# VectorE takes GpSimd's elementwise work, and the first half's low-rank projection moves into its first two tiles

## The chip, the cores and the metric

One Trainium2 chip, one of its cores. The metric is the time of one execution on the device in microseconds (us): 1757.95 us is the median of three runs of the kernel before (1757.51 to 1762.42). The profile is one further execution, of 1757.43 us.

## What is computed

One layer of a hybrid decoder in float32, for a prompt of 1024 tokens with 16 meta tokens ahead, and for 8 sequences of 8 new tokens. Cut to what the change touches:

```python
def rmsnorm(x, w):
    var = jnp.mean(xf * xf, axis=-1, keepdims=True)
    return xf * lax.rsqrt(var + EPS) * w

h = rmsnorm(x, norm_pre)                                    # [tokens, 2048]
q_a, k_a, v_a, gate_a, q_g, k_g, v_g, gate_g, z_g = jnp.split(h @ w_in, SPLIT_POINTS, axis=-1)
log_f = jax.nn.log_sigmoid(z_g @ w_a2 + b_a) / GLA_NORMALIZER   # z_g: 16 columns, the low-rank projection
# (A) softmax attention in a window of 128, gated by silu(gate_a)
# (B) gated linear attention (GLA, 4 heads) with decays from log_f, normalised, gated by silu(gate_g)
x + rmsnorm(concat(A, B) @ w_out, norm_post)
```

The norm's factor 1/sqrt(var) belongs to a token, and so to a column of the transposed arrays that the kernel works on. It commutes with the projection: the kernel projects `x * norm_pre` and multiplies each result by the token's factor `rs`.

## The kernel before

**Layout and halves.** Activations are transposed: 128 features on the partitions, tokens on the free axis. Tokens fall into a first half (A, 512) and a second half (B, 592). `in_half` runs for A, then for B; the output projection follows for A (`out_first`) and for B (`out_second`, twice 296 columns).

**The projections.** `proj` (L343) makes one or two tiles of 128 output features. A tile is 16 contraction steps (kt) of three float32r matmuls at L358, because each operand is split in two parts, `whi`+`wlo` for the weights and `hh`+`hl` for the activations: `hh,whi`, `hl,whi`, `hh,wlo`. That is 48 matmuls a tile and column part. The activation parts of a half are made once, in the half's first `proj` call (`prep_x`, L215), which runs two tiles together: ScalarE makes `hh` (L201), VectorE `hl` (L202). The weights come in jobs of 8 kt (512 KB, tile `wraw`, 3 buffers). `convert` makes of each job two pieces of 4 kt: ScalarE casts `whi` (L322), VectorE subtracts for `wlo` (L324), 4 buffers each. `weights` keeps one job ahead of the one in use.

**The sum of squares.** In half A the same `prep_x` squares each x and adds it up in two sums, `acc[0]` for even kt and `acc[1]` for odd ones. GpSimd squares kt 0 and 1 (L229) and adds the even ones (L233), VectorE adds the odd ones (L233), ScalarE squares the others (L231). After the last matmul of the two tiles, `finish_norm` (L235) adds over the partitions on TensorE (L244), and `rstd` (L168) makes `rs`. Only then are the two tiles, q and k of the first GLA head, taken out of PSUM, multiplied by `rs` (`evac_rs`). Half B's sum is made during half A by `prepass` (L248), added on GpSimd (L259).

**The low-rank projection.** `zproj` (L368) then takes a weight job of its own, `wz` (304 KB), and makes 32 matmuls at L377 from all 16 `hh` and `hl`. Its result times `rs`, split again (`zT`), feeds the decays of every GLA head of the half (L671).

**What sets the order.** A scheduler places the program's instructions in each engine's queue; an engine works its queue off in that order and waits on semaphores. Attention (`attend`), GLA (`gla`) and side jobs (`setup_late`, `prepass`) are generators, of which `mid` and `end` run a step between projection calls, so their instructions lie between matmuls of L358. GpSimd's part of them before: the softmax's last multiplication (L529), the two multiplications of each level of a GLA head (`operands`, L737 and L738, after two exponentials of ScalarE), the last one of `silu` (L438), and those of L784, L812, L823 and L915. Its other work is memsets, copies of some columns, and six DMAs, among them two small-packet writes to DRAM for the bias tables (L140, L141).

## Time and profile before

| | |
|---|---|
| median of 3 runs | 1757.95 us (1757.51 to 1762.42) |
| the profiled execution | 1757.43 us, span 1755.6 us, mean granted TensorE clock 0.991 |
| TensorE busy, matmuls | 1716.6 us, 98% |
| TensorE busy, weight loads | 1552.1 us, 88% |
| VectorE busy | 1014.0 us, 58% |
| ScalarE busy | 741.9 us, 42% |
| GpSimd busy | 355.4 us, 20%, 332 instructions |

In the rows, PE is TensorE's matmuls, PEld its weight loads, DVE VectorE, ACT ScalarE, POOL GpSimd, SP the engine that issues the loads. A group's row gives line, engine, operation, out<-in tiles and shapes, count, busy time and mean duration, then the engine's idle time ahead of it and what ended that. A matmul's duration in the trace overlaps the next one's; the pace is read from one start to the next.

### The profile page before, as it was taken

Reading aid. Unit: us, or ns where it says so; the run is one execution under the profiler, and the core shown is the slowest. Engines: PE = TensorE matmul, PEld = TensorE weight load, DVE = VectorE, ACT = ScalarE, POOL = GpSimd, SP = SyncE. Lnnn points to the kernel's source line nnn. Section 1 sums busy time; section 2 is a strip of 40 time slices with the busy share of each in tenths; the row PEclk is TensorE's granted clock in tenths of the full one; section 3 lists DMA queues with packets and bytes.
Section 4 is the critical chain, followed back from the end, with each engine's and each line's share of the span. In section 5 each row is a group of like instructions: output and inputs, shape, how many; then the busy total and the mean of one; then the engine's idle time right before and its main releaser. Section 6 shows DMA issues by size and latency. Waiting matters only on the chain.

```text
span 1755.6 us, 28693 instructions
## 1 busy us (share of the span) xinstructions
PE 1716.6 (98%) x11068; PEld 1552.1 (88%) x11068; DVE 1014.0 (58%) x1993; ACT 741.9 (42%) x1603; POOL 355.4 (20%) x332
## 2 busy tenths in 40 slices
PE   7999999999999999999999999999999999999995
PEld 5778888888888999999999999999997788899995
DVE  7466675675656757435654564455656533585655
ACT  6344454353434534332443243343435333544442
POOL 3043253141114114211231022210521100000000
PEclk9999999999999999999999999999999999999998
DMA  6733433222233532313223231323225333686664
GB/s 212 146 97 111 132 115 105 93 83 94 88 96 108 175 121 70 101 64 113 82 67 102 81 115 60 102 77 107 79 77 199 104 99 102 224 262 222 208 217 159
DMA packets 85736, 213.61 MB, mean 122 GB/s; under 512 B 11504, under 2 KB 33936, under 8 KB 85568
## 3 DMA queue, kind: packets, MB, share of 16 engines
q1 hardware_dynamic: 82416, 204.90, 36.2%
q0 software_dynamic: 992, 4.46, 1.6%
q10 hardware_dynamic: 2192, 2.43, 0.4%
q8 instruction: 87, 1.43, 0.3%
q14 instruction: 49, 0.40, 0.1%
HBM read 186.32 MB, written 27.39 MB: 122 GB/s over the span
## 4 chain that ended last, share of the span: by engine, by line
PE 88%; DVE 4%; DMA 3%; ACT 2%; issue 1%; POOL 1%; SPq 0%; DVEq 0%; POOLq 0%; ACTq 0%
PE mm L358 76%; PE ps L521 2%; DMA wraw<-in_win 1%; PE ps L764 1%; PE ps L551 1%; PE ps L377 1%; PE ps L537 1%; PE ps L876 1%; DVE wlo L324 1%; PE ps L848 1%; PE ps L878 1%; PE ps L553 1%; ACT whi L322 0%; PE ps L187 0%; PE ps L923 0%
## 5 line engine op out<-in xcount | busy, mean ns | idle before, releaser
L358 PE MATMUL mm<-hh,whi 128*128 128x296 f32 (+2 forms) x2880 | 846.3, 333 | 8.5 <-ACT whi L322 6.0
L358 PE MATMUL mm<-hh,wlo 128*128 128x296 f32 (+2 forms) x2880 | 840.7, 331 | 2.6 <-DVE wlo L324 2.5
L358 PE MATMUL mm<-hl,whi 128*128 128x296 f32 (+2 forms) x2880 | 836.9, 330 | 2.1 <-DVE hl L202 1.6
L324 DVE TENSOR_TENSOR wlo<-wraw,whi 128x512 fp32r<-128x512 f32 x544 | 420.3, 778 | 444.4 <-ACT whi L322 432.1
L322 ACT CAST whi<-wraw 128x512 fp32r<-128x512 f32 x544 | 334.5, 619 | 785.6 <-PE mm L358 698.8
L358 PEld LDWEIGHTS mm<-hh,whi 128*128 128x128 f32 x2880 | 506.7, 189 | 51.5 <-ACT whi L322 7.7
L358 PEld LDWEIGHTS mm<-hh,wlo 128*128 128x128 f32 x2880 | 507.9, 189 | 43.0 <-DVE wlo L324 4.9
L358 PEld LDWEIGHTS mm<-hl,whi 128*128 128x128 f32 x2880 | 508.9, 189 | 39.6 <-DVE hl L202 3.1
L529 POOL TENSOR_TENSOR st<-st,den 128x512 f32<-128x512 f32 x32 | 44.3, 1386 | 350.0 <-ACT whi L322 260.3
L401 DVE TENSOR_TENSOR ft<-mm,rs 128x592 f32<-128x592 f32 (+2 forms) x60 | 43.6, 727 | 69.9 <-PE mm L358 67.2
L485 ACT ACTIVATE st<-st,nm 128x128 f32<-128x128 f32 (+1 forms) x140 | 54.7, 391 | 65.7 <-DVE nm L479 65.7
L737 POOL TENSOR_TENSOR ft<-ft 128x256 f32<-128x256 f32 (+2 forms) x48 | 53.0, 1104 | 142.1 <-ACT ft L735 142.1
L438 POOL TENSOR_TENSOR ft<-ft 128x496 f32<-128x496 f32 (+1 forms) x32 | 51.6, 1613 | 92.0 <-ACT ft L437 92.0
L738 POOL TENSOR_TENSOR ft<-ft 128x256 f32<-128x256 f32 (+2 forms) x48 | 50.0, 1041 | 1.4 <-ACT ft L736 1.4
L915 POOL TENSOR_TENSOR ft<-ft 128x496 f32<-128x496 f32 (+1 forms) x16 | 27.2, 1719 | 99.3 <-DVE ft L912 99.3
L540 DVE TENSOR_TENSOR pT<-ps,c_sides 128x512 f32<-128x512 f32 x64 | 41.3, 682 | 2.5 <-PE ps L537 2.3
L734 DVE TENSOR_TENSOR ft<-ft 128x512 f32<-128x512 f32 (+2 forms) x48 | 40.8, 859 | 0.0
L509 DVE TENSOR_TENSOR qst<-ft,qst 64x256 fp32r<-64x256 f32 x64 | 38.6, 603 | 2.5 <-ACT qst L508 0.6
L403 DVE SCALAR_TENSOR_TENSOR ft<-mm,rs 128x496 f32<-128x496 f32 (+1 forms) x24 | 17.4, 725 | 35.6 <-PE mm L358 35.4
L764 PEld LDWEIGHTS ps<-ft 128*126 128x126 f32 (+3 forms) x256 | 30.9, 187 | 6.1 <-POOL ft L738 4.6
L259 POOL TENSOR_TENSOR rs<-rs,ft 128x592 f32<-128x592 f32 x15 | 24.1, 1609 | 52.0 <-ACT ft L257 51.9
L764 PE MATMUL ps<-ft 128*126 128x64 f32 (+3 forms) x256 | 31.2, 267 | 3.2 <-POOL ft L738 3.2
(316 smaller groups left out, 1605.4 us busy)
## 6 DMA issues: line engine op xcount, KB each, us to landing
wraw<-in_win SPq DMA_DIRECT2D x174, 512.0 KB, 3.8
wraw<-in_wout SPq DMA_DIRECT2D x96, 512.0 KB, 4.4
ft<-in_xB SPq DMA_DIRECT2D x48, 296.0 KB, 4.2
ft<-mix SPq DMA_DIRECT2D x16, 296.0 KB, 6.3
ft<-in_xA SPq DMA_DIRECT2D x16, 256.0 KB, 5.6
ft<-in_state SPq DMA_DIRECT2D x16, 256.0 KB, 5.0
...
```

What stands on the lines that cost most here:

```text
L322: nc.scalar.copy(hi, r)
L324: nc.vector.tensor_tensor(lo, r, hi.bitcast(F32), ALU.subtract)
L358: nc.tensor.matmul(ps[:, j, :p1 - p0], w[:, k % 4, :], h[kt][:, p0:p1], start=(kt == 0 and a == 0), stop=(kt == KT - 1 and a == 2))
L401: self.nc.vector.tensor_tensor(o, src, r, ALU.mult)
L438: nc.gpsimd.tensor_tensor(x[:, :T], x[:, :T], t[:, :T], ALU.mult)
L485: nc.scalar.activation(s, s, AF.Exp, bias=nm[:R, j:j + 1], accum_out=den[:R, j:j + 1])
L529: nc.gpsimd.tensor_tensor(st, st, den.rearrange("p (v t) -> p v t", v=2).unsqueeze(3).to_broadcast([P, 2, 2, P]), ALU.mult)
L540: nc.vector.tensor_tensor(sb[:, j], pt, self.sides[:, j:j + 1].to_broadcast([P, 4, P]), ALU.mult)
L734: nc.vector.tensor_tensor(ev, bv, bv[:, :, h - 1:h].to_broadcast([P, ns, 2 * h]), ALU.subtract)
L737: nc.gpsimd.tensor_tensor(ev[:, :, h:], qv[:, :, h:], ev[:, :, h:], ALU.mult)
L738: nc.gpsimd.tensor_tensor(ev[:, :, :h], kv[:, :, :h], ev[:, :, :h], ALU.mult)
L764: nc.tensor.matmul(ps[:P - h, j * 64:(j + 1) * 64], xs[:, :P - h], xs.rearrange("p (s e) -> p s e", e=2 * h)[:, :, h:], start=True, stop=True)
```

## The change

All elementwise arithmetic of GpSimd (L259, L438, L501, L529, L613 to L618, L723, L724, L737, L738, L784, L812, L823, L902, L915) goes to VectorE, one word each. GpSimd keeps memsets, copies and its DMAs. In half A's first call, ScalarE makes all 16 squares, and VectorE adds them up at least three steps of kt behind (`add_square`). The weights of the low-rank projection are loaded once more at the start, ahead of x 2, and converted at once into buffers that are free then. Half A's first call becomes `first`: its two tiles carry the 32 matmuls of the low-rank projection as a third sum, two kt behind. The tiles q and k are copied out raw; the norm is finished within the next tile (v0), between its two jobs, and q, k and z are multiplied by `rs` then. Half B keeps the old form. In the diff, the engine's name alone changes in some 20 more places like the first.

```diff
@@ prepass
-                nc.gpsimd.tensor_tensor(acc[:, :T], acc[:, :T], x[:, :T], ALU.add)
+                nc.vector.tensor_tensor(acc[:, :T], acc[:, :T], x[:, :T], ALU.add)
...
@@ prep_x
-                a = self.acc[kt % 2][:, :T]
-                if kt < 2:
-                    nc.gpsimd.tensor_tensor(a, x[:, :T], x[:, :T], ALU.mult)
-                else:
-                    nc.scalar.activation(x[:, :T], x[:, :T], AF.Square)
-                    eng = nc.vector if kt % 2 else nc.gpsimd
-                    eng.tensor_tensor(a, a, x[:, :T], ALU.add)
+                sq = self.acc[kt] if kt < 2 else x
+                nc.scalar.activation(sq[:, :T], x[:, :T], AF.Square)
+                if kt >= 2:
+                    self.sqs.append((kt, x))
+                if len(self.sqs) > 3:
+                    self.add_square(T)
...
@@ start
+            if j == 0:
+                wz = self.sm([P, 2, 4, P], "pT", 1).rearrange("p a b c -> p (a b) c")
+                self.load_x(A, 2)
+                nc.sync.dma_start(out=wz.rearrange("p k m -> p (k m)")[:, :608], in_=self.i["wz"])
             self.load_x(A, 4 + 4 * j)
+        self.wz0 = self.convert_z(wz, [self.sm([P, 4, P], "A", 1).bitcast(F32R).rearrange("p k m -> p (k m)"),
+                                       self.sm([P, 2, 256], "qst", 1, F32R).rearrange("p k m -> p (k m)")])
...
@@ proj
+                if extra is not None:
+                    extra(kt)
             if c == 0:
+                if between is not None:
+                    between()
                 self.mid()
-        if pre is not None and name == "win" and H.i == 0:
-            self.finish_norm(H)
...
@@ first (new)
+        zs = self.ps()
+        lag = 2
+        def extra(kt):
+            if kt >= lag:
+                self.zstep(H, self.wz0, [zs], kt - lag)
+            if kt == KT - 1:
+                for k in range(KT - lag, KT):
+                    self.zstep(H, self.wz0, [zs], k)
...
+        self.proj(H, "win", [base, base + 1], [evac("q", o0, nc.scalar.copy), evac("k", 0, nc.vector.tensor_copy)],
+                  [H.asked, H.parts], pre=lambda kts: self.prep_x(H, kts), extra=extra)
...
+        def between():
+            self.finish_norm(H)
+            self.zfinish(H, [zs])
+            nc.vector.scalar_tensor_tensor(q[:, o0:T], q[:, o0:T], scale, self.rs[:, o0:T], op0=ALU.mult, op1=ALU.mult)
+            nc.vector.tensor_tensor(k[:, :T], k[:, :T], self.rs[:, :T], ALU.mult)
+            self.glas.append(self.gla(H, 0, self.zT, io))
...
+        self.proj(H, "win", [base + 2], [evac_v], between=between)
```

**TensorE, the last kt of the first two tiles.** Before, the two tiles end, and the sum of squares (L244) and the first two of 32 matmuls of the low-rank projection (L377) follow:

```order
L358 MATMUL mm<-hh,wlo 128x496
L358 MATMUL mm<-hh,whi 128x512
L358 MATMUL mm<-hl,whi 128x512
L358 MATMUL mm<-hh,wlo 128x512
L244 MATMUL ps<-st,ones 128x512 x2
L377 MATMUL ps<-hh,whi 128x512
L377 MATMUL ps<-hl,whi 128x512
```

Now, over one kt near the end of the two tiles (L377 is here the line of the tiles, L403 that of the low-rank projection, `qst` its converted weights):

```order
L403 MATMUL ps<-hh,qst 128x512
L403 MATMUL ps<-hl,qst 128x512
L377 MATMUL mm<-hh,whi 128x496
L377 MATMUL mm<-hl,whi 128x496
L377 MATMUL mm<-hh,wlo 128x496
L377 MATMUL mm<-hh,whi 128x512
L377 MATMUL mm<-hl,whi 128x512
L377 MATMUL mm<-hh,wlo 128x512
L403 MATMUL ps<-hh,qst 128x512
```

The low-rank matmuls stand among the tiles' own from the seventh place of the queue on; after the last kt six of them follow, then v0. The sum of squares stands in the middle of v0 (L251).

**VectorE, the same two tiles.** Before, from kt 7 to kt 13 (L202 `hl`, L324 `wlo`, L233 sum of squares):

```order
L202 SCALAR_TENSOR_TENSOR hl<-ft,wpre,hh 128x512
L324 TENSOR_TENSOR wlo<-wraw,whi 128x512 x2
L233 TENSOR_TENSOR st<-st,ft 128x512
L202 SCALAR_TENSOR_TENSOR hl<-ft,wpre,hh 128x512 x3
L233 TENSOR_TENSOR st<-st,ft 128x512
L202 SCALAR_TENSOR_TENSOR hl<-ft,wpre,hh 128x512 x3
```

Now, from kt 7 to kt 12 (L238 sum of squares, L343 `wlo`):

```order
L202 SCALAR_TENSOR_TENSOR hl<-ft,wpre,hh 128x512
L343 TENSOR_TENSOR wlo<-wraw,whi 128x512 x2
L238 TENSOR_TENSOR st<-st,ft 128x512 x2
L202 SCALAR_TENSOR_TENSOR hl<-ft,wpre,hh 128x512 x3
L238 TENSOR_TENSOR st<-st,ft 128x512
L202 SCALAR_TENSOR_TENSOR hl<-ft,wpre,hh 128x512
L238 TENSOR_TENSOR st<-st,ft 128x512
L202 SCALAR_TENSOR_TENSOR hl<-ft,wpre,hh 128x512
```

VectorE's queue holds 14 additions in place of 7. Of the 14, ten stand ahead of the last `hl`, against six of the 7 before.

**VectorE, the start of the first GLA head.** Before, VectorE had these between `wlo` pieces, and GpSimd the multiplications of the levels:

```order
L324 TENSOR_TENSOR wlo<-wraw,whi 128x512
L734 TENSOR_TENSOR ft<-ft 128x512
L324 TENSOR_TENSOR wlo<-wraw,whi 128x512
L786 TENSOR_TENSOR ft<-ft 128x512
L401 TENSOR_TENSOR ft<-mm,rs 128x496
```

Now (L764 is the old L734, L767 and L768 the multiplications of a level, L468 that of `silu`):

```order
L343 TENSOR_TENSOR wlo<-wraw,whi 128x512
L751 TENSOR_TENSOR ft<-ft 128x256
L753 TENSOR_TENSOR ft<-ft 128x256
L764 TENSOR_TENSOR ft<-ft 128x512
L814 TENSOR_TENSOR ft<-ft 128x512
L754 TENSOR_TENSOR ft<-ft 128x256
L466 SCALAR_TENSOR_TENSOR ft<-ft 128x496
L767 TENSOR_TENSOR ft<-ft 128x128x2
L768 TENSOR_TENSOR ft<-ft 128x128x2
L816 TENSOR_TENSOR ft<-ft 128x512
L468 TENSOR_TENSOR ft<-ft 128x496
L343 TENSOR_TENSOR wlo<-wraw,whi 128x512 x3
```

Ten instructions now stand between two `wlo` pieces on VectorE's queue.

## Rows read from the trace of the kernel before

**Rows 1.** The page's first part: busy time, share of the span, instructions.
```profile
span 1755.6 us, 28693 instructions
PE 1716.6 (98%) x11068; PEld 1552.1 (88%) x11068; DVE 1014.0 (58%) x1993; ACT 741.9 (42%) x1603; POOL 355.4 (20%) x332
```

**Rows 2.** Waits of TensorE's matmuls, whole span: us in total, times, longest.
```profile
PE mm L358 <- ACT whi L322: 6.0, 2, 5.8
PE ps L764 <- POOL ft L738: 3.2, 4, 1.3
PE ps L537 <- POOL st L529: 0.9, 2, 0.6
```

**Rows 3.** Timeline of TensorE, first 47 us: start, duration, instruction, wait before.
```profile
5.83 0.78 PE L358 MATMUL mm<-hh,whi 128*128 128x496 f32 x1 [5.83 <-ACT whi L322]
...
14.92 0.40 PE L358 MATMUL mm<-hh,whi 128*128 128x512 f32 x1
15.15 0.39 PE L358 MATMUL mm<-hl,whi 128*128 128x512 f32 x1
...
26.97 0.50 PE L358 MATMUL mm<-hl,whi 128*128 128x496 f32 x1 [1.62 <-DVE hl L202]
...
28.23 0.61 PE L358 MATMUL mm<-hh,whi 128*128 128x496 f32 x1
28.64 0.61 PE L358 MATMUL mm<-hl,whi 128*128 128x496 f32 x1
...
37.35 1.88 PE L244 MATMUL ps<-st,ones 128*128 128x512 f32 x4
38.67 0.80 PE L377 MATMUL ps<-hh,whi 128*128 128x512 f32 x1
...
46.51 0.40 PE L358 MATMUL mm<-hh,whi 128*128 128x512 f32 x1
```

**Rows 4.** Stretches: us; PE, PEld, DVE, ACT, POOL busy; clock, DMA share, GB/s.
```profile
8.00:14.00 6.00, 5.58 (x13) 4.11 (x14) 5.18 (x7) 5.68 (x11) 1.94 (x3) 1.00 0.98 365
14.00:22.00 8.00, 8.00 (x35) 6.38 (x33) 7.97 (x10) 6.31 (x11) 3.50 (x2) 1.00 0.94 357
22.00:28.00 6.00, 3.76 (x15) 2.31 (x15) 5.96 (x7) 4.79 (x8) 3.26 (x2) 1.00 0.32 92
28.00:32.00 4.00, 4.00 (x12) 3.13 (x11) 4.00 (x7) 3.28 (x7) 2.32 (x1) 0.57 0.20 57
```

**Rows 5.** Timeline of VectorE and GpSimd in the start.
```profile
15.74 1.68 POOL L233 TENSOR_TENSOR st<-st,ft 128x512 f32<-128x512 f32 x1 [3.78 <-ACT ft L231]
16.29 1.68 DVE L233 TENSOR_TENSOR st<-st,ft 128x512 f32<-128x512 f32 x1
...
30.78 2.44 DVE L202 SCALAR_TENSOR_TENSOR hl<-ft,wpre,hh 128x512 fp32r<-128x512 f32 x2
```

**Rows 6.** Groups by line and shape: POOL, DVE and ACT.
```profile
L529 POOL TENSOR_TENSOR st<-st,den 128x512 f32<-128x512 f32 x32 | 44.3, 1386 | 350.0 <-ACT whi L322 260.3 <-DVE den L487 89.7
L737 POOL TENSOR_TENSOR ft<-ft 128x256 f32<-128x256 f32 x36 | 37.1, 1030 | 116.9 <-ACT ft L735 116.9
L804 DVE TENSOR_TENSOR ft<-ft 128x512 f32<-128x512 f32 x8 | 5.5, 693 | 0.3
L556 DVE TENSOR_TENSOR ft<-ps,ft 128x256 f32<-128x256 f32 x24 | 10.1, 422 | 1.1 <-PE ps L553 1.1
L322 ACT CAST whi<-wraw 128x512 fp32r<-128x512 f32 x544 | 334.5, 619 | 785.6 <-PE mm L358 698.8 <-issue 28.5 <-DMA wraw<-in_wout 21.4
L324 DVE TENSOR_TENSOR wlo<-wraw,whi 128x512 fp32r<-128x512 f32 x544 | 420.3, 778 | 444.4 <-ACT whi L322 432.1 <-PE ps L537 5.4 <-PE ps L521 3.5
```

**Rows 7.** Two stretches of 10 us with much DVE and POOL work, columns as in 4.
```profile
120.00:130.00 10.00, 8.19 (x64) 6.21 (x62) 8.91 (x15) 4.72 (x11) 8.78 (x10) 1.00 0.23 62
180.00:190.00 10.00, 10.00 (x52) 8.46 (x51) 9.89 (x24) 4.72 (x15) 5.85 (x4) 1.00 0.28 97
```

**Rows 8.** The chain that ended last, at its longest load: start, us, what.
```profile
55.38 19.91 DMA wraw<-in_win
```

More of the change, by code (lines that the diff above doesn't have):

```diff
@@ L219, in prep_x @@
             self.acc = [self.sm([P, W], "st", 2), self.sm([P, W], "st", 2)]
+            self.sqs = []
             self.load_x(H, KT)
@@ L225, in prep_x, with add_square @@
             if H.i == 0:
[L227 to L233 removed]
+                sq = self.acc[kt] if kt < 2 else x
[4 more added lines that the diff above has]
+                    self.add_square(T)
+    def add_square(self, T):
+        kt, x = self.sqs.pop(0)
+        a = self.acc[kt % 2][:, :T]
+        self.nc.vector.tensor_tensor(a, a, x[:, :T], ALU.add)
     def finish_norm(self, H):
@@ L237, in finish_norm @@
         T, n = H.T, H.n
+        while self.sqs:
+            self.add_square(T)
         self.rs = self.sm([P, W], "rs", 2)
@@ L264, in stream @@
     def stream(self):
-        for _ in range(2):
+        for half in range(2):
             for u in range(4):
@@ L274, in stream @@
                     yield from (("win", f, c) for c in range(2) for f in cols[:2])
-                    yield "wz", 0, 0
+                    if half:
+                        yield "wz", 0, 0
                     cols = cols[2:]
@@ L306, in convert @@
         if name == "wz":
-            raw = raw.rearrange("p k m -> p (k m)")[:, :608]
-            nc.sync.dma_start(out=raw, in_=self.i["wz"])
-            out = []
-            for j in range(2):
-                hi = self.wp.tile([P, 4, P], F32R, name="whi", bufs=4).rearrange("p k m -> p (k m)")[:, :352]
-                nc.scalar.copy(hi, raw[:, 256 * j:256 * j + 352])
-                rv, wv = (t.rearrange("p (k m) -> p k m", m=32) for t in (raw[:, 256 * j:256 * j + 256], hi[:, :256]))
-                nc.vector.tensor_tensor(wv[:, :, 16:32], rv[:, :, 0:16], wv.bitcast(F32)[:, :, 0:16], ALU.subtract)
-                out.append(hi)
-            return out
+            nc.sync.dma_start(out=raw.rearrange("p k m -> p (k m)")[:, :608], in_=self.i["wz"])
+            return self.convert_z(raw, [self.wp.tile([P, 4, P], F32R, name="whi", bufs=4).rearrange("p k m -> p (k m)")
+                                        for _ in range(2)])
         out = []
@@ L341, in weights, with proj @@
         return got
-    def proj(self, H, name, fs, evacs, cols=None, pre=None):
+    def proj(self, H, name, fs, evacs, cols=None, pre=None, extra=None, between=None):
         nc = self.nc
@@ L374, in zproj, with zstep, zfinish @@
         for kt in range(KT):
-            for a, h in enumerate((self.hh, self.hl)):
-                for j in range(H.np):
-                    nc.tensor.matmul(pss[j][:, :n], w2[kt // 8][:, 32 * (kt % 8):32 * (kt % 8) + P], h[kt][:, j * n:j * n + n],
-                                     start=(kt == 0 and a == 0), stop=(kt == KT - 1 and a == 1))
+            self.zstep(H, w2, pss, kt)
+        self.zfinish(H, pss)
+    def zstep(self, H, w2, pss, kt):
+        n = H.n
+        for a, h in enumerate((self.hh, self.hl)):
+            for j in range(H.np):
+                self.nc.tensor.matmul(pss[j][:, :n], w2[kt // 8][:, 32 * (kt % 8):32 * (kt % 8) + P],
+                                      h[kt][:, j * n:j * n + n], start=(kt == 0 and a == 0), stop=(kt == KT - 1 and a == 1))
+    def zfinish(self, H, pss):
+        nc = self.nc
+        n = H.n
         z = self.ft()[:32]
@@ L500, in attend @@
             first = self.sm([P, 2, P], "first", 1)
-            nc.gpsimd.tensor_tensor(first, bias, self.neg.unsqueeze(1).to_broadcast([P, 2, P]), ALU.add)
+            nc.vector.tensor_tensor(first, bias, self.neg.unsqueeze(1).to_broadcast([P, 2, P]), ALU.add)
         def parts(p):
@@ L955, in end, with first, evac, f @@
         self.tick(self.side)
+    def first(self, H, base, scale, io):
+        nc = self.nc
+        o0, T = H.o0, H.T
+        zs = self.ps()
[6 more added lines that the diff above has]
+                    self.zstep(H, self.wz0, [zs], k)
+        def evac(key, c0, copy):
+            def f(ps):
+                t = io[key] = self.ft()
+                copy(t[:, c0:T], ps[:, 0, :T - c0])
+            return f
+        self.proj(H, "win", [base, base + 1], [evac("q", o0, nc.scalar.copy), evac("k", 0, nc.vector.tensor_copy)],
+                  [H.asked, H.parts], pre=lambda kts: self.prep_x(H, kts), extra=extra)
+        q, k = io["q"], io["k"]
+        self.blank(H, q)
+        def between():
[4 more added lines that the diff above has]
+            self.glas.append(self.gla(H, 0, self.zT, io))
+        self.end()
+        t = self.ft()
+        io["v0"] = t
+        def evac_v(ps):
+            self.evac_rs(H, t)(ps)
+        self.proj(H, "win", [base + 2], [evac_v], between=between)
     def in_half(self, H):
@@ L976, in in_half @@
                     self.proj_ft(H, base + j, scale if j == 0 else None, io, key)
-            for i in range(2):
+            for i in range(1 if H.i == 0 and u == 0 else 0, 2):
                 self.proj_ft(H, base + 2 + i, None, io, "v%d" % i)
```

57 lines of the change are left out of this document (35 added, 22 removed).

## The prediction

> **What bounds the kernel now.** I read the page's busy shares first, then TensorE's waits, then the start in stretches and in time, then the groups by line. TensorE's matmuls fill 98% of the span [rows 1], so whatever the change does elsewhere, it pays only where TensorE waits or runs at half pace. There is little of that: 39 us of the span pass without a matmul [rows 1], the first 5.83 among them [rows 3]. The list of waits has two kinds that the change touches: some on GpSimd, at the levels of the GLA heads (L764) and at the softmax (L537), 3.2 + 0.9 = 4.1 us together [rows 2], and those of the start. There TensorE begins at 5.83 us and reaches the tile v0 at 46.51 [rows 3]. In between lie 96 matmuls of the two tiles, the sum of squares and 32 low-rank matmuls. At full pace a matmul starts 0.23 us after the one before (14.92 to 15.15), so 128 take 29.4 us, and the sum of squares takes 1.32 (37.35 to 38.67) [rows 3]: 30.8 us of work in 40.7 us. The 9.9 us lost are seen in rows 4: few matmuls up to 14 us, while loads come in (13 in 6 us); 2.2 us without any in 22 to 28 us, where VectorE is busy for 5.96 of 6 us and TensorE waits for its `hl` (1.62 us at 26.97) [rows 3, 4]; and after that stop a granted clock of 0.57, where a matmul takes 0.41 us (28.23 to 28.64) [rows 3, 4], that is mostly the 1.2 GHz level.
>
> Why VectorE is late there: a VectorE addition that starts during a GpSimd addition on the same kind of operands takes 1.68 us and ends after it, where an undisturbed operation of that shape takes 0.69 [rows 5, 6]. Its last two `hl` took 2.44 us together, to 33.2 us [rows 5].
>
> **The change, part by part.** *The start.* The low-rank matmuls are the same 32, but they now stand among the 96, so they fill waits and leave the path behind them. The walk: ScalarE has a square ahead of its first weight cast, one pass of about 0.62 us [rows 6]; the cast waited for its load before, so I take 0.3 us for the later first matmul. The extra 304 KB come ahead of x 2, at 365 GB/s 0.8 us [rows 4], while TensorE is short of x anyway. Before, TensorE had started 16 matmuls by 14.0 us, 13 of them from 8 us on [rows 4]; I take the same number, with some of them now low-rank ones. The other 112 at 0.23 us end at 14.0 + 0.3 + 25.8 = 40.1 us, provided VectorE is ahead. Its queue up to the last `hl` holds from 8.3 us on 15 `hl`, 9 `wlo` and 10 additions, 34 x 0.69 us [rows 6], and two small pieces of 0.3: it ends at 32.4 us. ScalarE, one pass of 0.62 each for 16 `hh`, the squares and the casts, is about two us ahead of it. TensorE needs that `hl` as its 118th matmul, at 14.3 + 102 x 0.23 = 37.8 us, 5 us later. So TensorE sets the end of the start, and no stop comes from 14 us on. With the sum of squares (1.3, now inside v0) the same point is reached at 41.4 in place of 46.5: 5.1 us. I take 4.5, as full pace may begin up to a microsecond later when the waits for x fall elsewhere. Bounds: 6 (the early waits filled as well) and 2 (a stop and a stretch at half pace as at 28 us remain).
>
> The rest of this edit I cost at nothing. The raw copies of q and k (one ScalarE, one VectorE pass) free the PSUM buffers that v0 and v1 need; nine matmuls, 2.1 us, lie between the last one of q and v0, and a cast and a copy take 1.24. The two multiplications by `rs`, 1.4 us of VectorE, lie inside v0 and v1. Without that cover each would cost at most its own pass.
>
> *GpSimd's waits.* The steps that TensorE waits for are chains of ScalarE exponentials and two multiplications of 1.03 us on GpSimd; VectorE does that shape in 0.42 [rows 6]. The softmax's step falls from 1.39 to 0.69. From 120 to 130 us GpSimd is busy for 8.78 us and TensorE has matmuls for only 8.19 [rows 7], so there GpSimd is the bound. Of the 4.1 us I take 3 off; bounds 0 and 4.1.
>
> *VectorE's load.* GpSimd's 355 us [rows 1] would take between 0.41 (0.42 to 1.03) and 0.5 (0.69 to 1.39) of that on VectorE: 146 to 178 us. Something comes back: `wlo` has a mean of 0.778 us against 0.69 undisturbed, 544 x 0.088 = 48 us [rows 6], and other lines with two SBUF inputs gain alike, 0 to 40. VectorE goes from 1014 to between 1072 and 1144 us, 61 to 65% of the span. I take 1080, near the low end, as the slow pairs of rows 5 are of other lines too. What counts is whether `wlo` comes in time. Its four buffers hold pieces of 12 matmuls, so a buffer that TensorE frees is needed again three pieces later, 3 x 12 x 0.23 = 8.3 us; cast and subtraction take 0.62 + 0.69, so 7.0 us are left. The ten instructions that now stand between two pieces at the first GLA head are five of 0.42 and five of 0.69, 5.6 us. Inside the lead, so 0; bounds 0 and +3.
>
> *Loads.* The writes of the bias tables stretch one weight load to 19.9 us [rows 8]. They still come when TensorE has as many jobs loaded, and the small table now goes out first, so the loads that wait for it on SP's queue find it landed. 0; bounds -0.8 and +2. After 1400 us GpSimd has no busy slice on the page, so nothing changes there.
>
> Sum: -4.5 - 3 = -7.5 us on the profiled execution's 1757.43 us gives 1749.9. The median of the runs lies 0.5 above that execution, so the forecast is **1750.5 us**.
>
> **Two rules of the Trainium skill.** That the slow pairs of rows 5 are a matter of order fits the page SBUF — State Buffer, section Who interferes with whom: a VectorE instruction with two SBUF inputs and a GpSimd one that reads SBUF take an exclusive lock in turns, and the second blocks fully. Rows 5 agree (the VectorE one ended 0.55 us behind GpSimd's), and by this rule VectorE's load would hardly rise. Against the change speaks the page Perfetto Trace Analysis, section Optimizing Scalar/DVE Operations: with VectorE saturated, moving work off it, even to GpSimd, may make sense. By that, with nothing given back, VectorE would stand at 1014 + 178 = 1192 us and the start would gain nothing from the move. The same section warns that the two share a read port.
>
> **The rivals.** *The start alone pays.* GpSimd's waits come back as waits for VectorE, whose queue now has `wlo` and the chains one behind the other: for it, that DVE is busy for 8.91 of 10 us where GpSimd was the bound [rows 7]; against it, the chain's shorter steps. Time 1757.95 - 4.5 + 0.5 = 1754. Chance 0.30.
>
> *VectorE's bursts make `wlo` late: slower.* From 180 to 190 us VectorE is busy for 9.89 us and GpSimd for 5.85 [rows 7]; at 0.5 that is 12.8 us of work in 10 us if nothing were given back, 2.8 us late. One such burst fits in the lead of 7.0 us; it decides if two or three follow each other without a pause, or if a chain that waits for ScalarE holds up the queue at its head. If the 16 runs of levels (8 heads and halves, two bursts each) cost 1 us each, the time is 1757.95 - 4.5 + 16 = 1769.5. Against it: VectorE idles 432 us for `whi` [rows 6], that is, for buffers that TensorE has yet to free. Chance 0.07.
>
> *The change doing nothing* is no case of its own: GpSimd's queue falls to 65 rows, and the low-rank matmuls stand in their new places.
>
> **How the numbers follow.** About 0.3% (5.3 us) is what a measurement of this kernel can tell from no change, so faster begins below 1752.7 and slower above 1763.2. The forecast has 0.63; its terms at their bounds give 1747 at best (-6, -4.1, -0.8) and with half of the start's gain or of the waits' missing 1753. So nearly all of it is faster: 0.58, and with a little of the first rival 0.60. The rest of the two is the same, 0.33; slower has 0.07. The range, 1746 to 1757, takes in the first rival with 3 us of new waits; it leaves out the second and some of the worst bounds.
>
> **What would show it.** In the profile after: TensorE reaches v0 near 40 us, without a wait for `hl` after 20 us and without a clock below 1 at 28 us; `wlo` with a mean near 0.69 us; VectorE near 1080 us busy; no wait for POOL at L794 (the old L764), and waits for DVE there of under 1 us in all. I am wrong on the start if v0 begins after 43 us, on the waits if those for VectorE in the GLA levels add up to 3 us, and on the load if waits of L377 for `wlo` grow by more than 3 us.

## The result, and the profile after

The changed kernel takes 1735.03 us (median of 4 runs, 1733.57 to 1739.12) against 1757.73 us for the kernel before, beside it on the same chip (4 runs, 1750.8 to 1762.42): a ratio of 0.9877, with a 95% interval from 0.986 to 0.9895. Run once more in the study (E8) it gave 0.9892, 0.9871 to 0.9913. It is faster by 20 to 23 us; the forecast was 7.5 us, and its range ended at 1746. The direction was right, the size was not.

The first part of the page, the kernel after:

```profile
span 1737.3 us, 28391 instructions
PE 1707.8 (98%) x11068; PEld 1548.7 (89%) x11068; DVE 1044.6 (60%) x2264; ACT 742.2 (43%) x1606; POOL 17.9 (1%) x60
```

Beside [rows 1], GpSimd has lost 337.5 us of work and VectorE gained only 30.6. The span is 18.3 us shorter in this execution, which was the slowest of the four.

TensorE's list of waits (us in total, times, longest), kernel after:

```profile
PE mm L377 <- ACT whi L341: 7.3, 2, 6.7
PE mm L377 <- DVE wlo L343: 1.5, 5, 0.4
PE ps L581 <- DVE pT L570: 0.8, 1, 0.8
```

The waits for GpSimd of [rows 2] are gone, and no waits for VectorE have come in their place at the GLA levels (now L794). Most of the first row (6.7 us) is the wait for the first load.

The start in TensorE's timeline (start, duration, instruction, wait before), kernel after:

```profile
6.65 0.78 PE L377 MATMUL mm<-hh,whi 128*128 128x496 f32 x1 [6.65 <-ACT whi L341]
...
39.02 0.39 PE L403 MATMUL ps<-hl,qst 128*128 128x512 f32 x1
39.25 0.40 PE L377 MATMUL mm<-hh,whi 128*128 128x512 f32 x1
...
44.81 1.88 PE L251 MATMUL ps<-st,ones 128*128 128x512 f32 x4
```

The tile v0 begins at 39.25 us; before it was 46.51 [rows 3]. The sum of squares (L251) now stands inside v0.

The same stretches as [rows 4], kernel after:

```profile
8.00:14.00 6.00, 5.59 (x16) 3.97 (x16) 4.78 (x9) 5.96 (x12) 0.00 (x0) 1.00 1.04 390
14.00:22.00 8.00, 8.00 (x36) 6.54 (x36) 8.00 (x14) 8.00 (x15) 0.11 (x1) 1.00 1.05 405
22.00:28.00 6.00, 6.00 (x29) 4.94 (x28) 6.00 (x10) 5.46 (x10) 0.00 (x0) 1.00 0.25 100
28.00:32.00 4.00, 4.00 (x19) 3.28 (x18) 3.04 (x6) 3.01 (x5) 0.00 (x0) 1.00 0.52 147
```

The stop between 22 and 28 us is gone (29 matmuls in place of 15), and with it the half-pace stretch behind it: 19 matmuls in 4 us at a granted clock of 1.00, not 12 at 0.57.

**Where the time came from.** The program takes its projection tiles out of PSUM in the same order in both kernels (L401 and L403 before, L431 and L433 after). The end of such an instruction (its start plus its duration in VectorE's timeline) is a landmark: v0's ends at 59.43 + 0.69 = 60.1 us before and 53.44 + 0.69 = 54.1 after. The differences add up to the gain of the two profiled executions:

| landmark | before | after | gain | of it since the last |
|---|---|---|---|---|
| v0 taken out | 60.1 | 54.1 | 6.0 | 6.0 |
| behind the first GLA head | 161.1 | 152.2 | 8.9 | 2.9 |
| in the second half | 961.3 | 951.0 | 10.3 | 1.4 |
| behind the 8 sequences' attention | 1150.3 | 1137.3 | 13.0 | 2.7 |
| behind a level at 1256 us | 1268.6 | 1252.4 | 16.2 | 3.2 |
| last one | 1323.2 | 1306.2 | 17.0 | 0.8 |
| span | 1755.6 | 1737.3 | 18.3 | 1.3 |

So 6.0 us are the start's, near the forecast's 4.5. The other 12.3 us stand where the forecast had 3. Between the second and third landmark lay 214 of GpSimd's 355 us before (161 to 961 us), and taking them away gave only 1.4 us: it pays at few places.

**The place at 1256 us** shows one of them whole. The wait in TensorE's timeline, and stretches (columns as in [rows 4]) of the kernel before:

```profile
1258.37 1.05 PE L764 MATMUL ps<-ft 128*120 128x64 f32 x8 [1.34 <-POOL ft L738]
```

```profile
1256.00:1260.00 4.00, 2.66 (x23) 2.44 (x24) 2.20 (x6) 0.00 (x0) 4.00 (x6) 1.00 0.40 104
1260.00:1264.00 4.00, 4.00 (x21) 4.00 (x20) 0.08 (x2) 0.00 (x0) 1.09 (x2) 0.57 0.94 334
```

and of the kernel after, at the same work:

```profile
1240.00:1244.00 4.00, 4.00 (x42) 3.66 (x41) 3.40 (x8) 1.86 (x5) 0.00 (x0) 1.00 0.38 131
1244.00:1248.00 4.00, 4.00 (x32) 3.90 (x32) 2.50 (x8) 0.00 (x0) 0.00 (x0) 1.00 0.17 66
```

A level waited 1.3 us for GpSimd (the longest of the four in [rows 2]). Behind that stop the granted clock stood at 0.57 for 4 us, mostly the 1.2 GHz level, with 21 matmuls where the like stretch after has 32. The list of waits had 1.3 us here; what was paid was 3.2: between the fourth and the fifth landmark the kernel before takes 118.3 us, the change 115.1.

The other runs' profiles bear this out. E2 and E3 have the same wait of 1.3 us, then 4 us at 0.60 and 0.58, and take 118.3 us too. In E4, E6 and E9, also with the levels on GpSimd, the same wait is 0.3, 0.6 and 0.6 us, the clock stays at 1.00, and they take 115.7 to 116.0 us. The wait and the stretch in E6:

```profile
1255.34 1.05 PE L794 MATMUL ps<-ft 128*120 128x64 f32 x8 [0.60 <-POOL ft L768]
```

```profile
1255.00:1259.00 4.00, 3.66 (x28) 3.56 (x29) 0.80 (x4) 0.00 (x0) 3.05 (x5) 1.00 0.90 292
```

So a wait of 0.6 us cost 0.8, and one of 1.3 us, with the half pace behind it, 3.2.

**The 8 sequences' attention** is another. Kernel before:

```profile
1060.00:1068.00 8.00, 7.92 (x65) 5.94 (x65) 3.43 (x6) 3.70 (x13) 2.05 (x6) 0.86 0.01 2
1068.00:1076.00 8.00, 8.00 (x44) 7.40 (x44) 5.62 (x15) 2.07 (x3) 3.25 (x5) 0.71 0.16 36
```

Kernel after:

```profile
1049.00:1057.00 8.00, 8.00 (x74) 6.39 (x73) 4.35 (x18) 5.49 (x18) 0.00 (x0) 0.99 0.21 57
1057.00:1065.00 8.00, 8.00 (x48) 7.41 (x49) 5.87 (x17) 1.26 (x3) 0.29 (x1) 0.80 0.14 43
```

TensorE's list has no wait at all here (1040 to 1090 us), yet in these two profiles the clock falls deeper and for longer before the change. The place differs from profile to profile, however. In the change's second profile (E8) the clock does not fall:

```profile
1056.00:1064.00 8.00, 8.00 (x67) 7.41 (x66) 5.68 (x16) 1.23 (x3) 0.29 (x1) 1.00 0.29 86
```

Between the third and the fourth landmark E8 takes 184.6 us, the change's first profile 186.3, the kernel before 189.0. The runs with this attention's multiplications on GpSimd (before, E2, E3, E4, E7) take 187.5 to 191.3, those with them on VectorE 184.4 to 187.5; at the upper end of these is E10, in which GpSimd multiplies nothing and the clock falls to 0.82 and 0.76 all the same. That GpSimd has a part in it is likely; the size, 2.7 us here, rests on single profiles.

**The first GLA head** is the third, with 2.9 us, and what the experiments turn on. TensorE's waits from 60 to 150 us, kernel before, the first two rows:

```profile
PE ps L764 <- POOL ft L738: 1.8, 3, 0.7
PE mm L358 <- DVE kf L401: 0.9, 1, 0.9
```

In VectorE's timeline L721 (L751 after) belongs to the first preparation of the head, and the first L734 (L764 after) to the next one, of level 1. Before:

```profile
83.99 0.42 DVE L721 TENSOR_TENSOR ft<-ft 128x256 f32<-128x256 f32 x1
...
111.96 0.69 DVE L324 TENSOR_TENSOR wlo<-wraw,whi 128x512 fp32r<-128x512 f32 x1 [0.79 <-ACT whi L322]
112.57 0.69 DVE L734 TENSOR_TENSOR ft<-ft 128x512 f32<-128x512 f32 x1
```

After:

```profile
84.58 0.42 DVE L751 TENSOR_TENSOR ft<-ft 128x256 f32<-128x256 f32 x1
84.92 0.42 DVE L753 TENSOR_TENSOR ft<-ft 128x256 f32<-128x256 f32 x1
85.25 0.68 DVE L764 TENSOR_TENSOR ft<-ft 128x512 f32<-128x512 f32 x1
```

L734 uses nothing that GpSimd makes; it reads what L721 has read before. VectorE idled between the `wlo` pieces of three tiles before it came: it stood behind them in the queue. With the seven multiplications of the head on VectorE, the scheduler queues the preparations together, 27 us earlier. Counted from the head's transposes, TensorE's levels then stand one or two to a tile (after 48, 48 and 48 matmuls of tiles), not all within one tile after 143.

### The profile page after: what moved, and what is told of

Read it like the earlier page. It is cut to its first block, busy times and chain, and to the rows that moved or that the text cites. A ratio compares the mean times of both kernels' runs of the same rounds, so it can differ in the third digit from the quotient of the medians.

```text
span 1737.3 us, 28391 instructions
## 1 busy us (share of the span) xinstructions
PE 1707.8 (98%) x11068; PEld 1548.7 (89%) x11068; DVE 1044.6 (60%) x2264; ACT 742.2 (43%) x1606; POOL 17.9 (1%) x60
## 4 chain that ended last, share of the span: by engine, by line
PE 92%; DMA 4%; DVE 2%; issue 1%; ACT 0%; SPq 0%; DVEq 0%; ACTq 0%
PE mm L377 78%; PE ps L551 2%; PE ps L794 2%; DMA wraw<-in_win 1%; PE ps L581 1%; PE ps L403 1%; PE ps L567 1%; DMA ft<-in_xB 1%; PE ps L878 1%; PE ps L906 1%; PE ps L908 1%; DMA st<-in_xA 1%; PE ps L583 1%; DMA ft<-in_xA 1%; PE ps L187 1%
## 5 line engine op out<-in xcount | busy, mean ns | idle before, releaser
L377 PE MATMUL mm<-hh,whi 128*128 128x296 f32 (+2 forms) x2880 | 844.2, 333 | 7.9 <-ACT whi L341 7.3
L377 PE MATMUL mm<-hh,wlo 128*128 128x296 f32 (+2 forms) x2880 | 837.8, 330 | 1.5 <-DVE wlo L343 1.5
L377 PE MATMUL mm<-hl,whi 128*128 128x296 f32 (+2 forms) x2880 | 836.9, 330 | 0.3 <-DVE hl L199 0.3
L343 DVE TENSOR_TENSOR wlo<-wraw,whi 128x512 fp32r<-128x512 f32 x544 | 370.8, 688 | 420.0 <-ACT whi L341 397.7
L377 PEld LDWEIGHTS mm<-hh,whi 128*128 128x128 f32 x2880 | 505.1, 189 | 50.2 <-ACT whi L341 7.7
L377 PEld LDWEIGHTS mm<-hh,wlo 128*128 128x128 f32 x2880 | 506.2, 188 | 41.7 <-DVE wlo L343 4.1
L377 PEld LDWEIGHTS mm<-hl,whi 128*128 128x128 f32 x2880 | 507.7, 189 | 37.7 <-issue 0.9
L431 DVE TENSOR_TENSOR ft<-mm,rs 128x592 f32<-128x592 f32 (+2 forms) x59 | 42.9, 727 | 64.9 <-PE mm L377 64.9
L515 ACT ACTIVATE st<-st,nm 128x128 f32<-128x128 f32 (+1 forms) x140 | 54.7, 392 | 49.6 <-DVE nm L509 49.5
L433 DVE SCALAR_TENSOR_TENSOR ft<-mm,rs 128x592 f32<-128x592 f32 (+1 forms) x23 | 16.7, 726 | 35.0 <-PE mm L377 34.7
L764 DVE TENSOR_TENSOR ft<-ft 128x512 f32<-128x512 f32 (+2 forms) x48 | 33.2, 703 | 0.0
L538 ACT CAST qst<-ft 64x256 fp32r<-64x256 f32 x64 | 25.9, 404 | 17.2 <-PE ps L551 13.7
L551 PE MATMUL ps<-kh,qst 128*128 128x256 f32 x128 | 32.6, 290 | 0.0
L794 PEld LDWEIGHTS ps<-ft 128*126 128x126 f32 (+3 forms) x256 | 31.0, 187 | 1.4 <-DVE wlo L343 0.2
L551 PE MATMUL ps<-kl,qst 128*128 128x256 f32 x128 | 31.1, 278 | 0.0
L794 PE MATMUL ps<-ft 128*126 128x64 f32 (+3 forms) x256 | 30.7, 266 | 0.0
L539 DVE TENSOR_TENSOR qst<-ft,qst 64x256 fp32r<-64x256 f32 x64 | 26.9, 420 | 3.1 <-ACT qst L538 1.2
L581 PE MATMUL ps<-pT,vt 128*64 128x128 f32 x256 | 27.3, 291 | 0.8 <-DVE pT L570 0.8
L202 DVE SCALAR_TENSOR_TENSOR hl<-ft,wpre,hh 128x512 fp32r<-128x512 f32 (+1 forms) x32 | 24.1, 787 | 6.1 <-ACT hh L201 6.1
L765 ACT ACTIVATE ft<-ft 128x256 f32<-128x256 f32 (+2 forms) x48 | 20.2, 422 | 17.5 <-DVE ft L764 17.4
```

The source lines that it names most:

```text
L343: nc.vector.tensor_tensor(lo, r, hi.bitcast(F32), ALU.subtract)
L377: nc.tensor.matmul(ps[:, j, :p1 - p0], w[:, k % 4, :], h[kt][:, p0:p1], start=(kt == 0 and a == 0), stop=(kt == KT - 1 and a == 2))
L431: self.nc.vector.tensor_tensor(o, src, r, ALU.mult)
L515: nc.scalar.activation(s, s, AF.Exp, bias=nm[:R, j:j + 1], accum_out=den[:R, j:j + 1])
L538: nc.scalar.copy(qs[d, v], qd)
L539: nc.vector.tensor_tensor(qs[o, v], qd, qs.bitcast(F32)[d, v], ALU.subtract)
```

## The experiments

Twelve runs. Medians of the kernel before beside them were 1756.84 to 1758.34 us. Landmarks are those of the table above, each from one profile:

| run | median us | ratio (95% interval) | v0 | first head | 2nd half | span |
|---|---|---|---|---|---|---|
| before | 1757.73 | | 60.1 | 161.1 | 961.3 | 1755.6 |
| the change | 1735.03 | 0.9877 (0.986 to 0.9895) | 54.1 | 152.2 | 951.0 | 1737.3 |
| E1 swap only | 1745.12 | 0.9932 (0.9908 to 0.9955) | 59.0 | 156.2 | 955.2 | 1739.2 |
| E2 start only | 1755.58 | 0.9996 (0.9977 to 1.0016) | 55.6 | 163.6 | 963.6 | 1759.0 |
| E3 squares only | 1754.88 | 0.9983 (0.9969 to 0.9998) | 55.3 | 156.2 | 956.4 | 1754.5 |
| E4 projection only | 1757.33 | 1.0001 (0.9984 to 1.0017) | 57.0 | 164.0 | 964.0 | 1757.7 |
| E5 change, projection in old place | 1739.24 | 0.9904 (0.9884 to 0.9924) | 55.6 | 153.4 | 952.2 | 1736.9 |
| E6 change, GLA on GpSimd | 1755.73 | 0.9987 (0.9973 to 1.0) | 55.2 | 163.8 | 962.8 | 1749.4 |
| E7 of the swap only GLA | 1749.01 | 0.9951 (0.9935 to 0.9968) | 54.8 | 152.9 | 952.9 | 1747.1 |
| E8 the change again | 1737.7 | 0.9892 (0.9871 to 0.9913) | 55.2 | 152.9 | 951.9 | 1736.4 |
| E9 E6, weights tied | 1753.81 | 0.998 (0.9969 to 0.9991) | 54.5 | 163.0 | 961.9 | 1751.1 |
| E10 change, level 1 tied late | 1742.62 | 0.9912 (0.9897 to 0.9926) | 55.5 | 156.3 | 955.3 | 1743.1 |
| E11 E6 in the change's order | 1745.23 | 0.9934 (0.992 to 0.9949) | 54.0 | 154.3 | 953.4 | 1739.4 |
| E12 change in E6's order | 1745.25 | 0.9941 (0.9926 to 0.9955) | 54.3 | 159.7 | 958.3 | 1742.0 |

### E1: the swap alone

```diff
-                nc.gpsimd.tensor_tensor(acc[:, :T], acc[:, :T], x[:, :T], ALU.add)
+                nc.vector.tensor_tensor(acc[:, :T], acc[:, :T], x[:, :T], ALU.add)
...
-            nc.gpsimd.tensor_tensor(ev[:, :, h:], qv[:, :, h:], ev[:, :, h:], ALU.mult)
+            nc.vector.tensor_tensor(ev[:, :, h:], qv[:, :, h:], ev[:, :, h:], ALU.mult)
```

(and so on: 16 lines, all but those of the start)

> All elementwise work of GpSimd on VectorE as in the change, but the start as in the kernel before: its squares partly on GpSimd, the low-rank projection in its old place. Theory A (GpSimd's work delayed far more than the 4.1 us of waits listed for it: along the profiled span, 9.5 of the 18.3 us came after 200 us): 9 to 13 us faster than before, about 1747, and wlo's mean near 0.69 us. Theory B (only the listed waits go, as predicted, and the rest of the gain is the start's or differs from run to run): 3 us faster, about 1754.5.

Measured: 12 us faster (1745.12 against 1757.12), theory A. Of the profiled gain 4.9 us come by the end of the first head, as the table shows, though the start still has its stop.

### E2, E3 and E4: the start alone, and its two parts

E2 is the change with the 16 lines back on GpSimd. E3 is the kernel before with this alone (and `add_square`, as in the change):

```diff
-                if kt < 2:
-                    nc.gpsimd.tensor_tensor(a, x[:, :T], x[:, :T], ALU.mult)
-                else:
-                    nc.scalar.activation(x[:, :T], x[:, :T], AF.Square)
-                    eng = nc.vector if kt % 2 else nc.gpsimd
-                    eng.tensor_tensor(a, a, x[:, :T], ALU.add)
+                sq = self.acc[kt] if kt < 2 else x
+                nc.scalar.activation(sq[:, :T], x[:, :T], AF.Square)
+                if kt >= 2:
+                    self.sqs.append((kt, x))
+                if len(self.sqs) > 3:
+                    self.add_square(T)
```

E4 is E2 with the old squares.

> The new start alone (squares on ScalarE, their additions on VectorE, low-rank projection inside the first two tiles); every other elementwise operation stays on GpSimd. Theory A (the start is worth what the landmarks settle at by 200 us): 8 to 9 us faster, about 1749. Theory B (the start is worth the 4.5 us predicted, and what more shows by 200 us came from the swap in the first GLA head): 4 to 5 us faster, about 1753. With the two parts independent, this gain and that of the swap alone add up to the 22 us of the change.

> Of the start only the squares: ScalarE makes all 16, VectorE adds them three steps behind; the low-rank projection and the finish of the norm stay in their old place, all other work stays on GpSimd. If the wait for hl near 25 us and the half-pace stretch behind it come from GpSimd's additions meeting VectorE's: both go, and 3 to 5 us are gained, about 1754. If VectorE's mere load is the cause (it gets 8 additions more): the wait stays or grows, and the time is that of before or 1 us more.

> Of the start only the low-rank projection: inside the first two tiles, norm finished in v0, q and k copied out raw; squares and additions partly on GpSimd as before, and all other elementwise work on GpSimd. If the moved matmuls fill the waits by themselves: 4 to 6 us faster, about 1753. If they pay only once VectorE is not held up by GpSimd: the wait for hl stays near 25 us, and the gain is under 2 us, about 1757.

Measured: E2 has no gain that stands clear of the spread (0.9977 to 1.0016), under both theories' 4 us by its median. E3 gains 2.2 us by the median, E4 nothing. The landmarks tell why. In E3 the stop and the half pace go, as its stretches show, and 4.9 us stay gained to the second half; at the 8 sequences' attention, where its clock falls to 0.59, 2.3 us of them are lost (191.3 us from the third landmark to the fourth, against 189.0):

```profile
22.00:28.00 6.00, 5.67 (x23) 3.65 (x22) 6.00 (x12) 5.89 (x11) 0.00 (x0) 1.00 0.17 44
28.00:32.00 4.00, 4.00 (x19) 3.29 (x18) 3.87 (x7) 1.72 (x4) 0.00 (x0) 1.00 0.66 208
```

In E4 TensorE has matmuls in all of 22 to 28 us, so the moved projection does fill that wait (0.8 us without come in the 4 us behind it):

```profile
22.00:28.00 6.00, 6.00 (x28) 4.98 (x27) 5.96 (x7) 4.24 (x7) 3.32 (x2) 1.00 0.30 105
```

Both E2 and E4 are ahead at v0, by 4.5 and 3.1 us, and 2.5 and 2.9 us behind the kernel before when the first head is done. TensorE's waits from 60 to 150 us, E2:

```profile
PE ps L187 <- ACT ft L815: 3.1, 1, 3.1
PE ps L794 <- POOL ft L768: 1.9, 3, 1.2
PE mm L377 <- DVE kf L431: 0.9, 1, 0.9
```

The start's gain is given back in the first GLA head, and more. The stop of 3.1 us ahead of the first level is new; neither E3 nor the kernel before has it. It stands where the projection is moved and GpSimd multiplies in the GLA heads; E3, with the same work on GpSimd and the projection in its old place, keeps its gain. E2's runs spread from 1750.26 to 1762.77 us and the profiled one (1760.83) is among the slowest, so its later landmarks may lie late; the same stop stands in E4's and E6's profiles.

### E5: the change with the projection in its old place

E3's squares and E1's swap together.

> All elementwise work on VectorE and the new squares, but the low-rank projection and the finish of the norm in their old place, behind the first two tiles. Theory A (of the start the squares pay; they took 4.9 us alone and kept them): the gains of the swap and of the squares add up, 4.9 + 4.9 us at 150 us where the whole change has 8.8, and the time is that of the whole change or a microsecond less, about 1734 to 1736. Theory B (the moved projection is what pays once nothing waits for GpSimd): 4 to 6 us slower than the whole change, about 1740.

Measured: 1739.24 us, ratio 0.9904, beside 1737.7 and 0.9892 for the change in the same session. The intervals overlap; up to the second half the landmarks put the projection's move at 0.4 to 1.5 us. Theory A holds in the place (first head done at 153.4 us, the change at 152.2 and 152.9), though the time is above its 1736; B's 4 to 6 us do not hold. Beside the new squares, the moved projection is worth next to nothing.

### E6 and E7: the seven GLA multiplications, or all the others

E6 is the change with these lines back on GpSimd; E7 has only these on VectorE:

```diff
-            nc.vector.tensor_tensor(e, kv[:, 0], qv[:, 1], ALU.mult)
-            nc.vector.tensor_tensor(e, e, w, ALU.mult)
+            nc.gpsimd.tensor_tensor(e, kv[:, 0], qv[:, 1], ALU.mult)
+            nc.gpsimd.tensor_tensor(e, e, w, ALU.mult)
...
-            nc.vector.tensor_tensor(ev[:, :, h:], qv[:, :, h:], ev[:, :, h:], ALU.mult)
-            nc.vector.tensor_tensor(ev[:, :, :h], kv[:, :, :h], ev[:, :, :h], ALU.mult)
+            nc.gpsimd.tensor_tensor(ev[:, :, h:], qv[:, :, h:], ev[:, :, h:], ALU.mult)
+            nc.gpsimd.tensor_tensor(ev[:, :, :h], kv[:, :, :h], ev[:, :, :h], ALU.mult)
```

(and those of L814, L842 and L853)

> The whole change, but the seven multiplications of the GLA heads (the pairs, the two of each level, and three more) stay on GpSimd. Theory A (the start's gain is given back in the first GLA head, at the waits for GpSimd): it is given back here too, 10 us or more slower than the whole change, 1746 or more, with a stop of about 3 us near 112 us and the stop with a half-pace stretch near 1250 us. Theory B (what counts is that GpSimd no longer holds up VectorE, wherever that is): half of the time taken from GpSimd stays gone, and about half of the swap's gain stays, 1740 to 1742.

> The whole change, but of the swap only the seven multiplications of the GLA heads go to VectorE; softmax, silu, the gates, the second half's squares and the rest stay on GpSimd. Theory A (GLA heads decide): within 3 us of the whole change, 1735 to 1738. Theory B (GpSimd holding up VectorE anywhere): 5 us or more slower than the whole change, 1740 or more.

Measured: E6 loses 18 us against the change by the medians, nearly all of its gain; 11.6 of them by the end of the first head, with a stop of 3.1 us, and no more up to the last landmark. That is theory A, but for the half-pace stretch near 1250 us, which did not come (a wait of 0.6 us, clock 1.00). E7 loses nothing there, but 11 us in all, which is theory B's number: 1.9 us by the second half, and 3.2 more at the 8 sequences' attention, whose multiplications are on GpSimd in E7 (the landmark behind it at 1142.4 us, the change's at 1137.3). Waits and stretches there, E7:

```profile
PE ps L661 <- POOL st L646: 0.3, 1, 0.3
PE ps L660 <- POOL st L648: 0.3, 1, 0.3
PE ps L659 <- POOL st L643: 0.2, 1, 0.2
```

```profile
1048.00:1056.00 8.00, 7.00 (x47) 5.18 (x46) 5.61 (x27) 5.23 (x24) 4.26 (x9) 1.00 0.01 5
1056.00:1064.00 8.00, 8.00 (x53) 6.29 (x51) 2.44 (x9) 3.15 (x7) 0.29 (x1) 0.65 0.11 29
```

Waits of 0.8 us for GpSimd, then a clock of 0.65 over 8 us: a small wait and then a low clock, as at 1256 us, though E10 shows a like one here without GpSimd. So neither theory alone: the GLA head decides up to 161 us, the other operations later.

### E8: the change again

> The whole change once more, for more of its runs beside the others on this chip and a second profile. If its first profile, 4 us above the median, was an ordinary run: a median within 2 us of 1735 and the same places of gain in time, with differences behind 1300 us. If the 22 us were partly luck of four runs: a median of 1738 or more.

Measured: 1737.7 us (1733.68 to 1742.72, 6 runs), between the two expectations. From 80 to 1052 us its landmarks lie 0.7 to 0.9 us behind the first profile's, from 1074 us on about 0.8 ahead. The gain is no luck of a few runs.

### E9 and E10: order or pace, first try

The first head has two explanations: GpSimd's multiplications are slow (1030 ns against 420 [rows 6]), or the order that the scheduler makes of them is bad. In E9, E6's next two weight subtractions are tied behind the head's preparations; in E10, the change's level 1 is tied behind the 13th weight subtraction after it. E9's tie:

```diff
+            if self.hold:
+                self.tc.add_manual_dep(sub.ins, self.hold.pop(), mybir.DependencyInfo(
+                    mybir.DependencyClass.NoSync, mybir.DependencyReason.DATA), reason="order")
```

> As the run with the GLA heads' seven multiplications on GpSimd, but in the first head the next weight subtractions are tied in VectorE's queue behind the head's first preparations, so that the levels of that head again stand one or two to a tile, about as in the whole change, instead of three tiles later and all within one tile. GpSimd does the same work as in that run. Theory A (order: what the swap gave at the first head, it gave because the scheduler then queues the preparations early): the 11.6 us lost by 150 us shrink to 3 or less, no stop over 1.5 us near 112 us, time 8 to 12 us under that run, 1744 to 1748. Theory B (pace: GpSimd's multiplications are too slow there): 8 us or more stay lost by 150 us, time 1752 or more.

> The whole change, all elementwise work on VectorE, but the first level's preparations of the first GLA head are tied behind the weight subtractions of the next three tiles, so that its levels stand behind 144 matmuls of tiles and then close together, as they did with GpSimd. Theory A (order): 6 to 11 us slower than the whole change, lost between 90 and 150 us, with a stop of 2 us or more near 112 us: 1744 to 1748. Theory B (pace): within 2 us of the whole change, 1735 to 1739.

Measured: E9 loses as much as E6 (163.0 us at the first head), but elsewhere. Stretches, E9:

```profile
80.00:90.00 10.00, 4.50 (x16) 2.59 (x14) 1.59 (x3) 5.57 (x11) 0.72 (x1) 0.89 0.70 191
```

The tie made weights wait behind a preparation that itself waits for GpSimd, just when a load was late: 16 matmuls in 10 us. It tells nothing of order and pace. E10 loses 3.3 us by the first head against E8, 4.9 by the medians (3.5 by the ratios to the kernel before beside each), between the two theories. Its level 1 stood one weight piece earlier than in E6, so the order was not quite E6's.

### E11 and E12: order and pace apart

Over some 430 instructions around the first head the queues of TensorE, ScalarE and VectorE are tied, each to a written list: E6's work in the change's order (E11), the change's work in E6's order (E12). GpSimd's instructions are free.

```diff
-        Kernel(tc, ins, outs, stack).run()
+        k = Kernel(tc, ins, outs, stack)
+        k.run()
+        by = {i.name: i for i in nc.cur_bb.bb.instructions}
+        for names in QUEUES:
+            for a, b in zip(names, names[1:]):
+                tc.add_manual_dep(by["I-%d" % b], "I-%d" % a, mybir.DependencyInfo(
+                    mybir.DependencyClass.NoSync, mybir.DependencyReason.DATA), reason="order")
```

> The same work as in the run with the GLA heads' seven multiplications on GpSimd, but over the first GLA head (some 420 instructions) the queues of TensorE, ScalarE and VectorE are tied to the very order that they have in the whole change; GpSimd's multiplications are the only ones that run elsewhere. Theory A (order): most of the 11.6 us lost by 150 us come back, 3 us or less stay lost; median 1746 or less. Theory B (GpSimd's pace): 8 us or more stay lost, in stops for GpSimd or for what queues behind it. The run that tied the weights could not tell, as its ties let weights wait for GpSimd.

> The whole change, all elementwise work on VectorE, but over the first GLA head the queues of TensorE, ScalarE and VectorE are tied to the order that they have with GpSimd (the levels three tiles later, then all within one tile). With the looser tie 3.3 us were lost by 150 us against the change's second profile. Theory A (order): 6 us or more are lost by 150 us, 3 of them in a stop before the first level near 112 us; median 1743 to 1746. Theory B (pace): 4 us or less.

Measured, at the end of the first head, against the change's 152.2 us:

| | the change's order | E6's order |
|---|---|---|
| VectorE multiplies | 152.2 (E8 152.9) | 159.7 (E12) |
| GpSimd multiplies | 154.3 (E11) | 163.8 (E6) |

Across, the order costs 7.5 or 9.5 us; down, GpSimd's pace costs 2.1 or 4.1 (with E8 for the change, 6.7 and 1.4 in place of 7.5 and 2.1). The medians agree: E11 is 10.5 us faster than E6 with the same multiplications on GpSimd, E12 7.6 slower than E8 with none on it (9.3 and 8.6 by the ratios). Theory A holds in both. No run ties the change to its own order, so what the ties alone cost is not known.

All four kernels of this table have the new start, and E6's order is not that of the kernel before. From v0's landmark to the head's the kernel before takes 101.0 us and E3 100.9, both with GpSimd multiplying and the preparation 52 us behind v0's landmark. E6 and E12 have it 62 and 59 us behind, and take 108.6 and 105.4; E11 takes 100.3, the change 98.1 (31 us behind). So the 7.5 to 9.5 us are what the moved projection would have lost with E6's order. They are no gain on the kernel before; that gain is 2.9 us. TensorE's waits from 60 to 150 us, the change:

```profile
PE mm L377 <- ACT whi L341: 0.6, 1, 0.6
```

That is the whole list. E11 has this one:

```profile
PE mm L382 <- ACT whi L346: 1.8, 1, 1.8
PE mm L382 <- DVE wlo L348: 0.9, 1, 0.9
```

There is no wait for GpSimd in either. E12, in which GpSimd multiplies nothing, has E2's stop:

```profile
PE ps L192 <- ACT ft L820: 3.1, 1, 3.1
PE mm L382 <- DVE kf L436: 0.9, 1, 0.9
```

Its VectorE timeline shows what the stop waits for:

```profile
112.25 0.69 DVE L348 TENSOR_TENSOR wlo<-wraw,whi 128x512 fp32r<-128x512 f32 x1 [2.03 <-ACT whi L346]
112.86 0.69 DVE L769 TENSOR_TENSOR ft<-ft 128x512 f32<-128x512 f32 x1
113.46 0.69 DVE L819 TENSOR_TENSOR ft<-ft 128x512 f32<-128x512 f32 x1
114.06 0.42 DVE L772 TENSOR_TENSOR ft<-ft 128x256 f32<-128x256 f32 x1
```

The preparation (L769, L819) begins only behind a weight piece at 112.25 us whose cast waits for a buffer of TensorE's, and VectorE was idle for 2.03 us before that piece.

## Why the prediction was wrong in size

**The start: right, a little small.** Forecast 4.5 us with a bound at 6; v0 at "near 40 us" (39.25), no wait for `hl` after 20 us (none in the list from 14 to 40 us), no clock below 1 at 28 us (1.00). Measured 6.0 at v0. The forecast put it down to the low-rank matmuls, provided that VectorE is ahead; the new squares alone bring v0 to 55.3 us (E3), 4.8 of the 6.0 us. What the forecast did not see is that with the moved projection this gain needs the order of the queues that the scheduler makes once the GLA heads leave GpSimd: E2, E4 and E6 have given it back by 161 us, E12 most of it, while E11 and E3, whose projection is in its old place, keep it.

**GpSimd's waits: the step that failed.** "Of the 4.1 us I take 3 off; bounds 0 and 4.1" priced the swap by the waits that the list names, with the queues as they were. Swapping alone measured 12 us (E1). By the profiles 12.3 us came behind v0 where the term had 3. The first head had 2.9 of them, about what the list names there (1.8 us for GpSimd at the levels, 0.9 for VectorE). Two things are missing from the term. First, the pace that TensorE loses behind a stop: 1.3 us of wait at 1256 us took 3.2 us. Second, a stretch in which the list has no wait, the attention of the 8 sequences: 2.7 us in these two profiles, a size that is not sharp. The other 3.5 us are spread (1.4, 0.8 and 1.3 in the table), and where they come from stays open.

The order of the queues was missing too. "The ten instructions that now stand between two pieces" were counted as a burden with a cost of 0 to +3; that the levels behind them come 27 us earlier was not asked. Without that order the new start's gain would have been lost: E2's first head ends at 163.6 us, the change's at 152.2, and E6, E11 and E12 put 7.5 to 9.5 of these 11.4 us down to the order. The forecast added the two gains up as if each came by itself; that the swap also brought the order in which they add up was luck.

**VectorE's load: right that it is covered, too high.** Forecast 1080 us (1072 to 1144), measured 1044.6. `wlo` fell to a mean near 0.69 us as foreseen:

```profile
L343 DVE TENSOR_TENSOR wlo<-wraw,whi 128x512 fp32r<-128x512 f32 x544 | 370.8, 688 | 420.0 <-ACT whi L341 397.7 <-PE ps L551 12.5 <-PE ps L567 6.4
```

That gave back 420.3 - 370.8 = 49.5 us [rows 6]. At the forecast's own rate of 0.41 the 337.5 us would be 138 on VectorE, and only 30.6 + 49.5 = 80 us are accounted for, so by this estimate other lines gave back some 58 us where it allowed 0 to 40. Two of them went from 38.6 to 26.9 us (L509, now L539) and from 40.8 to 33.2 (L734, now L764). This fits the Trainium skill's page SBUF — State Buffer, section Who interferes with whom, by which a VectorE instruction with two SBUF inputs and a GpSimd one that reads SBUF exclude each other. E6 and E7, with about half of GpSimd's work each, have means of 715 and 730 ns in between.

**Loads and bias tables: right.** The longest load took 21.3 us, against 19.9 [rows 8], but no wait of that kind over 0.6 us stands in the list from 60 to 150 us.

**The rivals.** "The start alone pays" is refuted: the swap alone pays 12 us (E1), the start alone 1.5, with an interval from a gain of 4 to a loss of 3 (E2), and the waits did not come back as waits for VectorE. "VectorE's bursts make `wlo` late" is refuted too: those waits add up to 1.5 us. Both rivals, and the forecast, left the queue order fixed.

**Still open.** Why the scheduler queues L734 so late when GpSimd has a part in the head was not tried; what it reads was there long before, and whether the buffer that it writes was free is not shown. Why the moved projection puts it later still (59 to 62 us behind v0's landmark in place of 52) was not tried either. Runs of one kernel spread by 5 to 14 us (the kernel before 1749.83 to 1764.24 in 29 runs), which no single profile shows; so E6's medians (18 us) and its profiles (12.1) differ, and so do E7's. The part of the gain behind 1323 us, 1.3 us in the profiles, is smaller than such differences.
